# A decoder trunk on one core: other pools for the first split weights, another order at the beginning, another PSUM bank for one head

## Chip, cores and metric

The kernel runs on one core of a Trainium2 chip. The metric is the device time of one execution in microseconds (us). PE is TensorE (matrix products), ACT is ScalarE, DVE is VectorE, POOL is GpSimd; SP issues most DMAs.

## What is computed

x is 512 x 1024 in float32; there are two layers, each of a feed-forward block, a mixer (retention beside attention with a forget gate) and another feed-forward block. The reference, cut:

```python
def swiglu(h, w_in, w_out):
    gu = h @ w_in
    a, b = gu[..., :D_FF], gu[..., D_FF:]
    return (jax.nn.silu(a) * b) @ w_out
...
def reference(x, ...):
    for l in range(DEPTH):                       # DEPTH = 2, D_FF = 2816
        x = x + 0.5 * swiglu(rmsnorm(x, norm_ffn1[l]), w_ffn1_in[l], w_ffn1_out[l])
        h = rmsnorm(x, norm_mix[l])
        x = x + mixing_sublayer(h, ...)          # 4 retention heads, 8 attention heads, two gates
        x = x + 0.5 * swiglu(rmsnorm(x, norm_ffn2[l]), w_ffn2_in[l], w_ffn2_out[l])
    return rmsnorm(x, norm_final)
```

## The kernel before

**Splits.** Every float32 product is done as three products of rounded parts: an operand is split into a high part (`split`, ACT cast, L154) and the rest (DVE subtraction, L155), and PE multiplies high by high, high by low and low by high. Weights come by DMA into staging tiles (`wst_A12`, `w0`, ...), and their two parts are `wH_i`, `wL_i`. For x scaled by a norm's gain the two parts are made by `scaled` (ACT L251, DVE L252).

**A feed-forward block's first product** goes in groups of columns (`ffn_group`), each by seven block products in place of eight. x^T lies as eight tiles x0 to x7 (feature blocks), and the forms are made from the pairs (x_k, x_k+4), k = 0 to 3, by `prep_forms`: `b2_k`, `n1_k` (each a scaled tile) and the last combinations `mh_k`, `ml_k` (high and low parts of four sums `mt`, DVE L273 to L281). The steps in order are A12 times b2 into the bank Y, A11 times n1 into X, S1A11 times a sum into X, S1 into W, S3 into X, S1A11A12 times b2 into W, A22 into X; for a group of four column blocks a step is 24 matmuls at L424. A step's weight has two halves with numbers of their own: wH_0 and wH_1 are A12's, wH_2 and wH_3 A11's, wH_4 and wH_5 S1A11's, wH_6 and wH_7 S1's.

**Buffers and order.** Tiles come from pools with a fixed number of buffers for each tag; within a tag the buffers go to the tiles in program order, and a tile waits until the reader of an older one is done. `wtile` takes every fourth split weight (wH_0, wL_0, wH_4, ...) from the tag `y` with four buffers, the others from `wH` and `wL`. The list FORM_TAGS (L246) gives the tags of the 14 form tiles in the order in which `prep_forms` makes them: the last two, mh3 and ml3, are in `y`. At the very beginning FIRST_TAGS (L247) holds instead; there mh1 and one b2 tile are in `y`. The program is written in order, and a scheduler then sets each engine's instruction queue, by priorities in program order and its own estimate of times; each engine runs its queue strictly in that order.

**The beginning.** `inputs` (from L1143) transposes x on PE and copies the result from PSUM with DVE (L1156). `ffn_plain` (L521 on) does the first two column blocks without the seven-product scheme: pa and pb on PE with the weights `wH_first`, each result multiplied by R, the 1/rms of every token laid out over 128 partitions (DVE L531, L540). R goes rT (PE, L302), rowsT (DVE, L304), a write to DRAM (r_d) and a read back (R), both issued by SP. `first_forms` after it makes the forms of the first block.

**The mixer's end.** `soft` and `weigh` do the attention heads: for head h the transposed probabilities ptr, then the values po (L193 to L195), whose bank `pos[h]` has one buffer (tag `po`); ACT and DVE split the result into o, after which the next head can use the bank. Gate products pg take a bank of the tag `acc` (three buffers), as many other products do, and `pyr`, `pyf` are the outputs of both branches. pw (L1107 adds it to x) ends the mixer; as each x_k is finished, `prep_forms` runs for the next block. There are three such passages into a feed-forward block with forms: mixer to second block in layer 0, second block of layer 0 to first block of layer 1, and mixer to second block in layer 1.

Of the kernel before, what the change touches and what calls it, by code (L numbers as in the profile page):

```python
# [14 lines left out]
P = 128  # L15
T = 512
# [4 lines left out]
DFF = 2816  # L21
# [5 lines left out]
FH = 8  # L27
# [15 lines left out]
def trunk(  # L43
# [25 lines left out]
    V, S, G, PE = nc.vector, nc.scalar, nc.gpsimd, nc.tensor  # L69
# [8 lines left out]
    def st(tag, name, dt=F32):  # L78
        return sp.tile([P, T], dt, tag=tag, bufs=SLOTS[tag], name=name)

    def st2(tag, name, dt=FR):

        return sp.tile([P, 2 * T], dt, tag=tag, bufs=PAIRS[tag], name=name)
# [5 lines left out]
    def wide(name, dt=F32):  # L89
        return sp.tile([P, 10 * P], dt, tag="wide", bufs=3, name=name)  # L90
# [4 lines left out]
    def pst(tag, bufs, name):  # L95
        return ps.tile([P, T], F32, tag=tag, bufs=bufs, name=name)

    def acc(name, other=False):
        return pst("lg", 2, name) if other else pst("acc", 3, name)
# [17 lines left out]
    def gain(n, l, m):  # L117
        c = (n * DEPTH + l) * KD + m
        return gcol[:, c:c + 1]

    def ngain(n, l, m):
        c = (n * DEPTH + l) * KD + m
        return ncol[:, c:c + 1]
# [24 lines left out]
    xs = [st("x", f"x{m}") for m in range(KD)]  # L148
# [4 lines left out]
    def split(src, hi, lo, lo_eng=None):  # L153
        S.copy(hi, src)  # L154
        (lo_eng or V).tensor_tensor(out=lo, in0=src, in1=hi.bitcast(F32), op=ALU.subtract)  # L155
# [63 lines left out]
    def square(src, i):  # L219

        sq = st("r" if i < 2 else "t", "sq")
        S.activation(sq, src, AF.Square)
        if i < 2:
            sqa[i] = sq
        else:
            G.dma_start(sqa[i % 2], sq, accum_op=ALU.add)
        if i == KD - 1:
            V.tensor_tensor(out=sqa[0], in0=sqa[0], in1=sqa[1], op=ALU.add)
# [14 lines left out]

    forms = {}

    FORM_TAGS = ("xh",) * 8 + ("o",) * 4 + ("y",) * 2  # L246
    FIRST_TAGS = ("o",) * 4 + ("y",) * 2 + ("v",) * 4 + ("qk",) * 4  # L247
    tags = [None]

    def scaled(h, lo, src, g):  # L250
        S.activation(h, src, AF.Copy, scale=g)  # L251
        V.scalar_tensor_tensor(  # L252
            out=lo, in0=src, scalar=g, in1=h.bitcast(F32), op0=ALU.mult, op1=ALU.subtract
        )

    def prep_forms(n, l, k, first=False):

        if k == 0:
            tags[0] = iter(FIRST_TAGS if first else FORM_TAGS)
            forms.clear()  # L260
        x1, x2 = xs[k], xs[k + 4]
        H2 = T // 2
        b2 = st2(next(tags[0]), f"b2_{k}")
        scaled(b2[:, 0:T], b2[:, T:2 * T], x2, gain(n, l, k + 4))
        if k % 2 == 0:
            forms["n1", k // 2] = st2(next(tags[0]), f"n1_{k}")
        n1 = forms["n1", k // 2][:, (k % 2) * T:(k % 2 + 1) * T]
        scaled(n1[:, 0:H2], n1[:, H2:T], x1[:, 0:H2], ngain(n, l, k))
        b1 = st("t", "b1")
        S.activation(b1, x1, AF.Copy, scale=gain(n, l, k))  # L270
        mt = wide("mt")[:, 0:2 * T]
        m1, m2, m3, m4 = (mt[:, i * H2:(i + 1) * H2] for i in range(4))
        V.tensor_tensor(out=m1, in0=b1[:, 0:H2], in1=b1[:, H2:T], op=ALU.subtract)  # L273
        V.scalar_tensor_tensor(
            out=m2, in0=x2[:, H2:T], scalar=gain(n, l, k + 4), in1=m1, op0=ALU.mult, op1=ALU.add
        )
        V.scalar_tensor_tensor(
            out=m3, in0=x2[:, H2:T], scalar=ngain(n, l, k + 4), in1=b1[:, H2:T],
            op0=ALU.mult, op1=ALU.add,
        )  # L280
        V.scalar_tensor_tensor(  # L281
            out=m4, in0=x2[:, 0:H2], scalar=gain(n, l, k + 4), in1=m2,
            op0=ALU.mult, op1=ALU.subtract,
        )
        mh, ml = st2(next(tags[0]), f"mh{k}"), st2(next(tags[0]), f"ml{k}")
        split(mt, mh, ml)
        for q in range(2):
            def at(t, c):
                return t[:, c + q * P:c + (q + 1) * P]
            forms["b21", k, q] = at(b2, 0), at(b2, T)  # L290
            forms["b22", k, q] = at(b2, H2), at(b2, T + H2)
            forms["n11", k, q] = at(n1, 0), at(n1, H2)
            for i in range(4):
                forms[f"m{i + 1}", k, q] = at(mh, i * H2), at(ml, i * H2)
        if not first:
            square(x1, 2 * k)
            square(x2, 2 * k + 1)

    def to_dram(cols, n, nm):

# [24 lines left out]
    def rpow(sums, count, nm):  # L325
        n = sums.shape[1]
        ms, r = small([P, n], f"ms{nm}"), small([P, n], f"rs{nm}")
        V.tensor_scalar(
            out=ms, in0=sums, scalar1=1.0 / count, scalar2=EPS, op0=ALU.mult, op1=ALU.add
        )  # L330
        G.tensor_tensor(out=r, in0=ms, in1=mhalf[:, 0:n], op=ALU.pow)
        return r
# [188 lines left out]
    def ffn_plain(w, mk):  # L521

        u, sil = [], []
        cha = mk(w, 0)
        rtok = rpow(sums(), D, "x")
        R = bcast(flat(to_dram(rtok, TB, "r")), "r", "R")
        for jj in range(2):
            o = acc("pa")
            proj(o, cha[jj], xH, xL)
            t = st("t", "t1")  # L530
            V.tensor_tensor(out=t, in0=o, in1=R, op=ALU.mult)  # L531
            s = st("p", "sil")
            S.activation(s, t, AF.Silu)
            sil.append(s)
        chb = mk(w, DFF, True)
        for jj in range(2):
            o = acc("pb", True)
            proj(o, chb[jj], xH, xL)
            t = st("t", "t2")
            V.tensor_tensor(out=t, in0=o, in1=R, op=ALU.mult)  # L540
            V.tensor_tensor(out=t, in0=t, in1=sil[jj], op=ALU.mult)
            h, lo = st(U_TAGS[jj], "uH", FR), st(U_TAGS[jj], "uL", FR)
            split(t, h, lo)
            u.append((h, lo))
        first_forms()
        return u, rtok

    def lazy(make):
# [189 lines left out]
    def mix(l):  # L738
        w = w_in[l]
# [110 lines left out]
        soft, pos = {}, {}  # L850
# [38 lines left out]
        def weigh(h, j):  # L889

            p, hh = h // 2, h % 2
            pr = soft[h][0]
            n = T - j * P
            pt = pst("pt", 2, "ptr")
            for i in range(j, TB):
                o0 = (i * (i + 1) // 2 + j) * P
                PE.transpose(pt[:, (i - j) * P:(i - j + 1) * P], pr[:, o0:o0 + P], ident)
            pH, pL = st("a", "pH", FR), st("a", "pL", FR)
            split(pt[:, :n], pH[:, :n], pL[:, :n])
            if j == 0:  # L900
                pos[h] = pst("po", 1, "po")
            po = pos[h]
            vs = slice(p * P, (p + 1) * P)
            mm3(
                po[:, j * P:], fvH[j][:, vs], fvL[j][:, vs], pH[:, :n], pL[:, :n],
                j == 0, j == TB - 1,
            )
            if j == TB - 1:
                if hh == 0:
                    oH[p], oL[p] = hl("o", "o")  # L910
                r = slice(hh * 64, hh * 64 + 64)
                split(po[r], oH[p][r], oL[p][r])
# [184 lines left out]
        for k in range(KD // 2):  # L1097
# [5 lines left out]
            for jj in range(2):  # L1103
                m = k + 4 * jj
                o = acc("pw", k % 2 == 1)
# [7 lines left out]
    def sums():  # L1113
        o = small([P, TB], "sumx")
        V.tensor_tensor(out=o, in0=ssx[:, 0:TB], in1=ssx[:, TB:2 * TB], op=ALU.add)
        return o
# [26 lines left out]
    def inputs():  # L1143
        for hf in range(2):
            xi = []
            for b in range(TB):
                t = st("g", "xi")
                load(t, x[0, b * P:(b + 1) * P, hf * T:(hf + 1) * T])
                xi.append(t)
            if hf == 0:  # L1150
                gains(0, DEPTH * KD, ((0, norm_ffn1),))
            for m in range(hf * 4, hf * 4 + 4):
                o = pst("pt", 2, "xT") if m % 2 else pst("lg", 2, "xT")
                for b in range(TB):
                    PE.transpose(o[:, b * P:(b + 1) * P], xi[b][:, (m % 4) * P:(m % 4 + 1) * P], ident)
                V.tensor_copy(xs[m], o)  # L1156
                xH[m], xL[m] = hl("xh", f"xh{m}")
                scaled(xH[m], xL[m], xs[m], gain(0, 0, m))
            for b in range(TB):
                sq = st("r", "sq")  # L1160
                c = hf * TB + b
                S.activation(sq, xi[b], AF.Square, accum_out=ssx[:, c:c + 1])

    def first_forms():
        for k in range(4):
            prep_forms(0, 0, k, True)

    inputs()
    for l in range(DEPTH):
# [61 lines left out]
```

## Time and profile before

| what | value |
|---|---|
| median of 3 runs (lowest to highest) | 2232.05 us (2231.32 to 2232.57) |
| the profiled execution | 2233.17 us, of it 2231.4 us from the first to the last instruction |
| PE busy | 2169.5 us (97%), mean granted clock 0.988 |
| DVE, ACT, POOL busy | 62%, 45%, 18% |
| idle PE before a step's first Y matmul | 39.5 us in 4 places |

The sum of a change is made against 2233.17 us, the time of the execution that the trace shows; it stands 1.1 us above the median. In a row of the timeline the time behind the start is the duration, and the bracket at the end is the engine's idle time before the row and what ended it. Rows of one engine overlap by some hundredths of a us, since an instruction's start is counted while the one before it drains. PEclk in a row of windows is the granted clock: 1.00 is 2.4 GHz and 0.50 is 1.2 GHz.

### The profile page before, as it was taken

The numbers are of one execution on the slowest core, as the hardware profiler recorded it, in microseconds if no ns is written. First come the engines' busy times: TensorE is split into PE (matmuls) and PEld (weight loads), VectorE is DVE, ScalarE is ACT, GpSimd is POOL, SyncE is SP. The second block draws the span as 40 slices with busy tenths as digits, with TensorE's granted clock in tenths as the row PEclk, the third lists the DMA queues.
The fourth block names the chain that finished last, engine by engine and source line by source line (L and its number), as shares of the span: only waits on it lengthen the run. The fifth ranks groups of instructions, "written<-read, shape, count | busy, mean of one in ns | idle before, by whom it ended". The sixth has DMA issues, their size and how long they took to land.

```text
span 2231.4 us, 26468 instructions
## 1 busy us (share of the span) xinstructions
PE 2169.5 (97%) x10199; PEld 1807.5 (81%) x10199; DVE 1378.7 (62%) x1928; ACT 998.0 (45%) x1439; POOL 395.8 (18%) x330
## 2 busy tenths in 40 slices
PE   5999999999999999999989999999999999999998
PEld 4888888888878788888868888888888787888887
DVE  6666574557854765757666574656577547747564
ACT  5444353345543453525544352543454435535343
POOL 1010001454231100001010000015532321000001
PEclk8999999999999999999999999999999999999999
DMA  9366335324253645747655564353332527536441
GB/s 272 95 176 183 106 84 146 100 76 114 95 130 102 161 128 137 193 118 188 163 138 154 139 162 117 85 152 90 95 91 95 151 77 202 164 105 170 132 114 67
DMA packets 232806, 293.77 MB, mean 132 GB/s; under 512 B 11252, under 2 KB 140120, under 8 KB 232680
## 3 DMA queue, kind: packets, MB, share of 16 engines
q1 hardware_dynamic: 203240, 239.12, 34.2%
q0 software_dynamic: 29440, 52.96, 14.0%
q8 instruction: 80, 1.31, 0.2%
q14 instruction: 46, 0.38, 0.1%
HBM read 282.03 MB, written 2.15 MB: 127 GB/s over the span
## 4 chain that ended last, share of the span: by engine, by line
PE 95%; DVE 2%; ACT 1%; DMA 1%; issue 1%; SPq 0%; POOLq 0%; ACTq 0%
PE X L424 21%; PE W L424 10%; PE po L194 6%; PE po L195 6%; PE po L193 6%; PE Y L424 5%; PE pg L195 3%; PE pg L193 3%; PE pg L194 3%; PE uT L503 2%; PE po L700 1%; PE po L702 1%; PE po L701 1%; PE prq L193 1%; PE pv L212 1%; PE pv L213 1%
## 5 line engine op out<-in xcount | busy, mean ns | idle before, releaser
L154 ACT CAST wH<-A 128x1024 fp32r<-128x1024 f32 x138 | 145.3, 1053 | 179.7 <-PE po L194 51.5
L155 DVE TENSOR_TENSOR wL<-A,wH 128x1024 fp32r<-128x1024 f32 x138 | 168.5, 1222 | 81.5 <-ACT wH L154 79.1
L424 PE MATMUL X<-wL,mh 128*128 128x512 f32 (+1 forms) x552 | 206.9, 375 | 0.0
L424 PE MATMUL X<-wH,ml 128*128 128x512 f32 (+1 forms) x552 | 206.9, 375 | 0.0
L194 PE MATMUL po<-uL,wH_o 128*128 128x512 f32 x528 | 206.8, 392 | 0.0
L195 PE MATMUL po<-uH,wL_o 128*128 128x512 f32 x528 | 203.7, 390 | 0.3 <-DVE wL_o L155 0.3
L424 PE MATMUL X<-wH,mh 128*128 128x512 f32 (+1 forms) x552 | 201.0, 376 | 0.0
L193 PE MATMUL po<-uH,wH_o 128*128 128x512 f32 x528 | 199.3, 392 | 0.0
L398 POOL DMA_DIRECT2D S<-in_w_ffn_in x71 | 80.4, 1198 | 607.7 <-DMA S<-in_w_ffn_in 362.8
L424 PE MATMUL Y<-wH,b 128*128 128x512 f32 (+1 forms) x368 | 114.3, 383 | 39.5 <-ACT wH L154 39.5
L154 ACT CAST wH_o<-wst_o 128x1024 fp32r<-128x1024 f32 (+1 forms) x72 | 70.5, 981 | 135.7 <-PE po L194 107.3
L155 DVE TENSOR_TENSOR wL_o<-wst_o,wH_o 128x1024 fp32r<-128x1024 f32 (+1 forms) x72 | 81.5, 1132 | 75.5 <-ACT wH_o L154 74.2
L155 DVE TENSOR_TENSOR wL<-wst_A,wH 128x1024 fp32r<-128x1024 f32 x77 | 93.8, 1222 | 46.9 <-ACT wH L154 46.3
L154 ACT CAST wH<-wst_A 128x1024 fp32r<-128x1024 f32 x77 | 80.6, 1051 | 86.8 <-PE Y L424 17.5
L424 PE MATMUL X<-wH,n 128*128 128x512 f32 (+1 forms) x368 | 119.4, 395 | 0.0
L424 PEld LDWEIGHTS X<-wH,mh 128*128 128x128 f32 x552 | 103.9, 188 | 19.1 <-ACT e L480 0.2
L424 PEld LDWEIGHTS X<-wL,mh 128*128 128x128 f32 x552 | 103.9, 188 | 18.9
L424 PEld LDWEIGHTS X<-wH,ml 128*128 128x128 f32 x552 | 103.9, 188 | 18.9
L195 PEld LDWEIGHTS po<-uH,wL_o 128*128 128x128 f32 x528 | 99.2, 188 | 20.9 <-DVE wL_o L155 0.7
L193 PEld LDWEIGHTS po<-uH,wH_o 128*128 128x128 f32 x528 | 99.1, 188 | 21.0 <-ACT uH L154 0.4
L194 PEld LDWEIGHTS po<-uL,wH_o 128*128 128x128 f32 x528 | 99.2, 188 | 19.8
L424 PE MATMUL W<-wH,b 128*128 128x512 f32 (+1 forms) x368 | 114.5, 375 | 0.0
(314 smaller groups left out, 5545.1 us busy)
## 6 DMA issues: line engine op xcount, KB each, us to landing
A<-in_w_ffn_in SPq DMA_DIRECT2D x84, 512.0 KB, 8.1
S<-in_w_ffn_in SPq DMA_DIRECT2D x47, 512.0 KB, 4.1
S<-in_w_ffn_in POOLq DMA_DIRECT2D x47, 512.0 KB, 7.7
wst_A<-in_w_ffn_in SPq DMA_DIRECT2D x45, 512.0 KB, 5.1
wst_o<-in_w_ffn_out SPq DMA_DIRECT2D x20, 1024.0 KB, 5.4
wst_g<-in_w_in SPq DMA_DIRECT2D x16, 1024.0 KB, 5.7
wst_S<-in_w_ffn_in SPq DMA_DIRECT2D x27, 512.0 KB, 5.9
wst_S<-in_w_ffn_in POOLq DMA_DIRECT2D x27, 512.0 KB, 7.4
```

The source lines that it names most:

```text
L154: S.copy(hi, src)
L155: (lo_eng or V).tensor_tensor(out=lo, in0=src, in1=hi.bitcast(F32), op=ALU.subtract)
L193: PE.matmul(o, wh, mh, start=first, stop=False)
L194: PE.matmul(o, wh, ml, start=False, stop=False)
L195: PE.matmul(o, wl, mh, start=False, stop=last)
L212: PE.matmul(o, mvH[kk][:, bs], h[:, k], start=kk == 0, stop=False)
L213: PE.matmul(o, mvH[kk][:, bs], lo[:, k], start=False, stop=False)
L398: G.dma_start(*piece(ts, r1, c1, s), accum_op=ALU.add)
L424: last_mm[0] = PE.matmul(*args, skip_group_check=True, **kw).ins
L503: PE.transpose(o[:, b * P:(b + 1) * P], ub[b][:, j * P:(j + 1) * P], ident)
L700: PE.matmul(o, uh, hh, start=k + i == 0, stop=False)
L701: PE.matmul(o, uh, ll, start=False, stop=False)
```

## The change

- FORM_TAGS and FIRST_TAGS: b2_0 and n1_0, the first forms, take `y`; the last combinations take `o`, at the beginning `qk`.
- `prep_forms` is cut into `prep_blocks` (b2, n1) and `prep_sums` (the combinations). At the beginning the second weight of `ffn_plain`, all four `prep_blocks` and two `prep_sums` stand ahead of R; the other two `prep_sums` stand behind the pb products.
- In `inputs` the odd x tiles are copied by ACT, the even ones by DVE as before.
- The values of the last head (h = 7) take a bank of `acc` in place of the one of `po`.

```diff
-    FORM_TAGS = ("xh",) * 8 + ("o",) * 4 + ("y",) * 2
-    FIRST_TAGS = ("o",) * 4 + ("y",) * 2 + ("v",) * 4 + ("qk",) * 4
+    FORM_TAGS = ("y",) * 2 + ("xh",) * 8 + ("o",) * 4
+    FIRST_TAGS = ("y",) * 2 + ("o",) * 4 + ("v",) * 4 + ("qk",) * 4
...
-    def prep_forms(n, l, k, first=False):
-
+    def prep_forms(n, l, k):
+
+        prep_blocks(n, l, k)
+        prep_sums(n, l, k)
+        square(xs[k], 2 * k)
+        square(xs[k + 4], 2 * k + 1)
+
+    def prep_blocks(n, l, k, first=False):
...
+    def prep_sums(n, l, k):
+        x1, x2 = xs[k], xs[k + 4]
+        H2 = T // 2
         b1 = st("t", "b1")
...
         cha = mk(w, 0)
+        chb = mk(w, DFF, True)
+        for k in range(4):
+            prep_blocks(0, 0, k, True)
+        for k in range(2):
+            prep_sums(0, 0, k)
         rtok = rpow(sums(), D, "x")
...
-        chb = mk(w, DFF, True)
...
-        first_forms()
+        for k in range(2, 4):
+            prep_sums(0, 0, k)
...
-                pos[h] = pst("po", 1, "po")
+                pos[h] = acc("po") if h == FH - 1 else pst("po", 1, "po")
...
-                V.tensor_copy(xs[m], o)
+                if m % 2:
+                    S.copy(xs[m], o)
+                else:
+                    V.tensor_copy(xs[m], o)
```

The order in which the engines run changes at these places. A name is the tile and its number in the program; `<-` stands between what is written and what is read.

ACT at the end of the mixer of layer 0, before; wH_0_6178 is the high part of A12's first half, mh3 the last combination:

```order
L251 ACTIVATE n1_2_6036<-x3_84,ncol_75 128x256
L270 ACTIVATE b1_6124<-x3_84,gcol_74 128x512
L222 ACTIVATE sq_6135<-x3_84 128x512
L154 CAST wH_3_6216<-wst_A11_0_6145 128x1024
L251 ACTIVATE b2_3_6119<-x7_88,gcol_74 128x512
L222 ACTIVATE sq_6138<-x7_88 128x512
L154 CAST mh3_6131<-mt_6126 128x1024
L154 CAST wH_0_6178<-wst_A12_0_6142 128x1024
```

The same engine in the changed kernel, where the cast of wH_0 stands now; wH_wo are weights of the products pw, and b2_1 is made from x5:

```order
L222 ACTIVATE sq_5964<-x1_82 128x512
L154 CAST mh0_5877<-mt_5872 128x1024
L154 CAST wH_wo2030_6059<-wst_wo203_6056 128x1024
L154 CAST wH_0_6178<-wst_A12_0_6142 128x1024
L251 ACTIVATE b2_1_5948<-x5_86,gcol_74 128x512
L222 ACTIVATE sq_5967<-x5_86 128x512
L154 CAST mh1_5960<-mt_5955 128x1024
L154 CAST wH_wo2031_6063<-wst_wo203_6056 128x1024
```

The cast of wH_0 moved from behind the last combination of x7 to a place ahead of b2_1, 19 instructions earlier: they are those from b2_1 to mh3.

PE between the values of head 4 (po_4799) and head 5 (po_4957) in layer 0, before; lg are logits, pg_5254 a gate product:

```order
L869 MATMUL lg_4961<-k0_4766,q_4690 128x256
L870 MATMUL lg_4961<-k0_4766,q_4690 128x256
L193 MATMUL pg_5254<-xh0_2568,wH_g0120_5246 128x512
L194 MATMUL pg_5254<-xh0_2568,wH_g0120_5246 128x512
L193 MATMUL po_4799<-pH_4876,v_3899 128x256
L195 MATMUL pg_5254<-xh0_2568,wL_g0120_5247 128x512
L193 MATMUL pg_5254<-xh1_2574,wH_g0120_5246 128x512
L194 MATMUL pg_5254<-xh1_2574,wH_g0120_5246 128x512
L195 MATMUL pg_5254<-xh1_2574,wL_g0120_5247 128x512
```

PE at the same place in the changed kernel:

```order
L884 MATMUL lg_4961<-k0_4766,q_4690 128x256
L885 MATMUL lg_4961<-k0_4766,q_4690 128x256
L193 MATMUL po_4799<-pH_4876,v_3899 128x256
L194 MATMUL po_4799<-pL_4877,v_3899 128x256
L195 MATMUL po_4799<-pH_4876,v_3899 128x256
L193 MATMUL po_4799<-pH_4896,v_3902 128x128
L912 MATMUL ptr_4948<-ident_72,pr5_4779 128x128 x4
L194 MATMUL po_4799<-pL_4897,v_3902 128x128
L195 MATMUL po_4799<-pH_4896,v_3902 128x128
L912 MATMUL ptr_4972<-ident_72,pr5_4779 128x128 x3
L912 MATMUL ptr_4994<-ident_72,pr5_4779 128x128 x2
```

The 48 matmuls of the two gate products pg_5254 and pg_5281 moved from here, and from between the values of heads 5 and 6, to a place behind the first matmul of head 7's values; the `acc` buffer of those values comes ahead of theirs in the program. pyr_5178, pyf_5192 and pyr_5212 moved up relative to them.

DVE at the beginning, before, around the copy rowsT and the first use of R (t1):

```order
L252 SCALAR_TENSOR_TENSOR xh7_190<-x7_88,gcol_74,xh7_190 128x512
L304 COPY rowsT_224<-rT_222 4x128
L155 TENSOR_TENSOR wL_first_299<-w0_288,wH_first_298 128x256
L155 TENSOR_TENSOR wL_first_299<-w0_289,wH_first_298 128x256
L155 TENSOR_TENSOR wL_first_299<-w0_290,wH_first_298 128x256
L155 TENSOR_TENSOR wL_first_299<-w0_291,wH_first_298 128x256
L531 TENSOR_TENSOR t1_255<-pa_230,R_228 128x512
```

DVE there in the changed kernel:

```order
L252 SCALAR_TENSOR_TENSOR b2_2_255<-x6_87,gcol_74,b2_2_255 128x512
L252 SCALAR_TENSOR_TENSOR n1_2_258<-x2_83,ncol_75,n1_2_258 128x256
L314 COPY rowsT_296<-rT_294 4x128
L252 SCALAR_TENSOR_TENSOR b2_3_261<-x7_88,gcol_74,b2_3_261 128x512
L252 SCALAR_TENSOR_TENSOR n1_2_258<-x3_84,ncol_75,n1_2_258 128x256
L155 TENSOR_TENSOR ml0_274<-mt_268,mh0_273 128x1024
L155 TENSOR_TENSOR ml1_285<-mt_279,mh1_284 128x1024
L546 TENSOR_TENSOR t1_327<-pa_302,R_300 128x512
L155 TENSOR_TENSOR wL_first_227<-w0_216,wH_first_226 128x256
```

rowsT now has eleven operations on forms, combinations and wL_0 ahead of it that it had not, and four copies of x less; ml0 and ml1 stand ahead of the first use of R, and the low part of the second pb weight (wL_first_227) moved behind it. The buffers of the S3 loads on SP are those of `w0`, the staging tiles that wL_first reads.

## Rows read from the trace of the kernel before

**Rows 1.** waits of PE: engine, line, releaser: us in total, times, longest us

```profile
PE Y L424 <- ACT wH L154: 39.5, 4, 19.9
PE po L193 <- DVE o L155: 4.8, 2, 2.4
PE pyf L193 <- ACT o L154: 1.3, 2, 0.7
```

**Rows 2.** windows, beginning: length; PE, PEld, DVE, ACT, POOL busy; PEclk; DMA share; GB/s

```profile
36.00:56.00 20.00, 0.10 (x1) 0.00 (x0) 18.29 (x30) 8.93 (x13) 4.08 (x5) 0.58 1.00 313
56.00:60.00 4.00, 3.97 (x10) 3.16 (x11) 4.00 (x8) 2.96 (x5) 2.08 (x3) 0.55 0.65 95
```

**Rows 3.** timeline of PE, beginning: start, us, line, operation, tiles, idle before

```profile
56.03 1.22 PE L424 MATMUL Y<-wH,b 128*128 128x512 f32 x2 [19.93 <-ACT wH L154]
...
86.44 0.39 PE L424 MATMUL W<-wH,b 128*128 128x512 f32 x1
86.67 0.39 PE L424 MATMUL W<-wL,b 128*128 128x512 f32 x1
```

**Rows 4.** timeline of ACT at the beginning

```profile
53.04 1.99 ACT L154 CAST mh<-mt 128x1024 fp32r<-128x1024 f32 x2 [5.81 <-DVE mt L281]
54.94 1.04 ACT L154 CAST wH<-wst_A 128x1024 fp32r<-128x1024 f32 x1
```

**Rows 5.** timeline of DVE at the beginning

```profile
25.81 0.27 DVE L304 COPY rowsT<-rT 4x128 f32<-4x128 f32 x1
...
37.39 1.29 DVE L531 TENSOR_TENSOR t<-pa,R 128x512 f32<-128x512 f32 x2 [5.91 <-DMA R<-r_d]
...
39.20 2.35 DVE L155 TENSOR_TENSOR wL<-wst_A,wH 128x1024 fp32r<-128x1024 f32 x2
...
45.94 0.47 DVE L277 SCALAR_TENSOR_TENSOR mt<-x,ncol,b 128x256 f32<-128x256 f32 x1
```

**Rows 6.** timeline of SP: the issues of R and of the S3 loads

```profile
32.87 0.34 SPq L102 DMA_DIRECT2D R<-r_d  x1
33.30 1.81 SPq L102 DMA_DIRECT2D S<-in_w_ffn_in  x4
```

**Rows 7.** timeline of PE at the first two passages into a feed-forward block

```profile
777.21 1.22 PE L424 MATMUL Y<-wH,b 128*128 128x512 f32 x2 [5.25 <-ACT wH L154]
...
1132.08 1.22 PE L424 MATMUL Y<-wH,b 128*128 128x512 f32 x2 [9.08 <-ACT wH L154]
```

**Rows 8.** windows behind the three passages

```profile
777.21:783.00 5.79, 5.79 (x14) 4.59 (x15) 4.42 (x4) 0.00 (x0) 0.00 (x0) 0.50 1.14 286
...
1132.08:1138.00 5.92, 5.92 (x14) 4.66 (x15) 2.86 (x3) 0.00 (x0) 0.00 (x0) 0.50 0.01 3
...
1874.04:1880.00 5.96, 5.96 (x16) 4.77 (x17) 4.42 (x4) 0.21 (x1) 1.98 (x2) 0.59 1.08 336
```

**Rows 9.** timeline of ACT at the mixer's end, layer 0

```profile
751.46 0.72 ACT L251 ACTIVATE b<-x,gcol 128x512 fp32r<-128x512 f32 x1
...
772.76 0.72 ACT L251 ACTIVATE b<-x,gcol 128x512 fp32r<-128x512 f32 x1
...
776.11 1.04 ACT L154 CAST wH<-wst_A 128x1024 fp32r<-128x1024 f32 x1
```

**Rows 10.** SP there, and DMA issues: tiles, queue, times, KB, median us to landing

```profile
747.93 10.88 SPq L102 DMA_DIRECT2D wst_A<-in_w_ffn_in  x4
wst_A<-in_w_ffn_in SPq DMA_DIRECT2D x4, 512.0 KB, 3.8
```

**Rows 11.** timeline of PE, first matmul of head 6's values, both layers

```profile
630.10 0.77 PE L193 MATMUL po<-pH,v 128*128 128x512 f32 x1 [2.39 <-DVE o L155]
...
1729.53 0.47 PE L193 MATMUL po<-pH,v 128*128 128x512 f32 x1 [2.39 <-DVE o L155]
```

**Rows 12.** windows behind those waits, layer 0 and layer 1

```profile
630.00:636.50 6.50, 6.40 (x20) 5.38 (x21) 5.20 (x24) 2.60 (x9) 0.00 (x0) 0.51 0.00 0
...
1730.00:1736.00 6.00, 5.84 (x33) 5.00 (x33) 4.97 (x26) 4.18 (x11) 0.00 (x0) 1.00 0.00 0
```

More of the change, by code (lines that the diff above doesn't have):

```diff
@@ L268, in prep_forms, with at @@
         scaled(n1[:, 0:H2], n1[:, H2:T], x1[:, 0:H2], ngain(n, l, k))
+        for q in range(2):
+            def at(t, c):
+                return t[:, c + q * P:c + (q + 1) * P]
+            forms["b21", k, q] = at(b2, 0), at(b2, T)
+            forms["b22", k, q] = at(b2, H2), at(b2, T + H2)
+            forms["n11", k, q] = at(n1, 0), at(n1, H2)
+    def prep_sums(n, l, k):
+        x1, x2 = xs[k], xs[k + 4]
+        H2 = T // 2
         b1 = st("t", "b1")
@@ L289, in at @@
                 return t[:, c + q * P:c + (q + 1) * P]
-            forms["b21", k, q] = at(b2, 0), at(b2, T)
-            forms["b22", k, q] = at(b2, H2), at(b2, T + H2)
-            forms["n11", k, q] = at(n1, 0), at(n1, H2)
             for i in range(4):
                 forms[f"m{i + 1}", k, q] = at(mh, i * H2), at(ml, i * H2)
-        if not first:
-            square(x1, 2 * k)
-            square(x2, 2 * k + 1)
     def to_dram(cols, n, nm):
@@ L1162, in inputs @@
                 S.activation(sq, xi[b], AF.Square, accum_out=ssx[:, c:c + 1])
-    def first_forms():
-        for k in range(4):
-            prep_forms(0, 0, k, True)
     inputs()
```

## The prediction

> **What bounds the kernel now.** PE is busy nearly all the time, so I read first where it waits. Of the table of its waits one line counts: Y at L424, the first matmul of a feed-forward block with forms, stood idle for 39.5 us in four places behind an ACT cast [rows 1]. The timeline gives the places: 19.93 us at the beginning [rows 3], 5.25 and 9.08 us at the first two passages [rows 7], and so 39.5 - 19.93 - 5.25 - 9.08 = 5.24 us at the third. Next come the values of the attention heads, 4.8 us in two places [rows 1, 11].
>
> Each wait on Y has a second price. In the stretch behind it the granted clock is 1.2 GHz: 0.50 over 5.79 us, 0.50 over 5.92 us and 0.59 over 5.96 us behind the three passages [rows 8], 0.55 in the 4 us behind the first wait [rows 2]. Work done there at half speed would have taken half of it: 2.9 + 3.0 + 2.4 = 8.3 us lost behind the passages.
>
> What ends the wait is wH_0, the cast of the first half of A12. ACT is not busy with other things: the cast stands behind mh3 in its queue, at 776.11 [rows 9], though its load was issued at 747.93 and took 3.8 us [rows 10]. It is the buffer that holds it back: wH_0 and wL_0 need two of the four `y` buffers, and mh3 and ml3 come first in the program. At the beginning the same holds with mh1: its sums were waited for 5.81 us on DVE, and wH_0 follows at 54.94 [rows 4]; DVE is 18.29 us busy in those 20 us [rows 2].
>
> **The passages.** In the new order wH_0 stands on ACT ahead of x5's b2, which began at 751.46 [rows 9]: 25 us earlier. What is late next? The last product pw ends PE's work at 777.21 - 5.25 = 771.96. Then 18 Y matmuls (k = 0 to 2) and 8 of X need nothing of x7, which is 26 matmuls of some 0.227 us (starts at 86.44 and 86.67 [rows 3]) = 5.9 us, to 777.9. x7's b2_3 began on ACT at 772.76 [rows 9] and needs the low part on DVE, some 3 us of DVE work (its sums, wL_3, its own), so about 776. The 48 matmuls of A12 and A11 last 10.9 us, to 782.8; S1A11's wH_4 needs the buffer of wH_0, free after the 15th matmul (775.4), a cast of 1.04 and a subtraction of 1.2 us, so 778 to 779, and mh3 and ml3 follow by 780. Nothing is late by this, at the first two passages within 0.3 us by the same reading. The load of A12 was the last thing that could hold the cast: 747.93 + 3.8 = 751.7 [rows 10], about when the cast's turn comes. ACT's queue behind it (b2_1, mh1, one pw weight) moves by the cast's 1.04 us, and ACT is idle for more than that before 772. The gain: 19.57 us idle and 8.3 us of clock, 27.9 us; with up to 1 us left at each passage, 24.5 to 28. I take **27.5 us**, since the cover (10.9 us) is twice what is late.
>
> **The beginning.** Here the bound changes hands. In the new order 12 Y matmuls stand among those of pa and pb, and x1 and x3 are copied by ACT ahead of the first weights, so PE starts pa some 1 us later (two copies of 0.6). PE was done with pb at 56.03 - 19.93 = 36.1 [rows 3], with the first pb 24 matmuls earlier, at 30.6; plus 1 and 12 x 0.227 us that is 34.4. rowsT stood at 25.81 [rows 5]; with eleven operations more (some 5.4 us by the starts of rows 5) and four copies of 0.6 fewer, and waits for ACT, it slips to 29 or 30. The second pb's low weight now stands on DVE behind t1, which waits for R. R's read was issued at 32.87 [rows 6], 7 us after rowsT, and had landed by 37.39 [rows 5]. If that time was the backlog of the DMA queues, R comes at about the same time; if it was the chain's own, 11.6 us from rowsT, it comes some 3.9 us later, at 41.3. I take the first: the small write stands behind weight loads, and these are issued as before. So PE is idle from 34.4 to about 38.4 (R, t1 and one quarter of wL_first).
>
> From R on DVE is the bound. Up to the low part of S1's first weight it has 16 operations of 512 columns (37.39: two in 1.29, some 0.6 each), 7 of 1024 (39.20: two in 2.35, some 1.13 each) and 12 of 256 (0.47, some 0.38 each) [rows 5]. By the spacing of starts that is 9.6 + 7.9 + 4.6 = 22.1 us, by durations 24.2: to 59.5 or 61.6. PE has 72 matmuls for that time (the second pb, the rest of A12, A11, half of S1A11), to 38.4 + 16.3 = 54.7, and waits again. From there 58 matmuls of S1A11, W and S3 follow, 13.2 us, to 72.7 or 74.8, with mh2, ml3 and the S3 weights ready in time: the S3 loads, issued at 33.30 [rows 6], now wait for wL_first, so some 6 us, and are first used at 67. Before, the same point is W's first matmul on b2 at 86.44 [rows 3]: 11.6 to 13.7 us gained. The second wait (5 us) will cost some clock, 0 to 3 us as behind the passages [rows 8]; the first one lies before a stretch that DVE bounds anyway. ACT's four copies and DVE's four fewer are in these starts. Ends: 6 (R late, clock lost) to 14. I take **12 us**.
>
> **The heads.** The change frees the bank between heads 6 and 7, where the trace shows no wait: 2.39 us stand before head 6's values, in both layers [rows 11]. It also takes 48 gate matmuls (10.9 us) from between heads 4 and 6 and puts them behind head 7's first one. A hand-over of the bank then costs PE 2.4 us twice (heads 4 to 5 and 5 to 6) in place of once, +2.4 us. Some comes back: the gates now stand where pyf waits, 0.65 us in each layer [rows 1], and where other small waits of some 0.6 us stand. Net +1.1 us a layer. The clock decides the rest: behind the same 2.39 us it was 0.51 over 6.50 us in layer 0 and 1.00 in layer 1 [rows 12], so one layer has lost 3.2 us already. Neither: 2.2 - 3.2 = -1 us; one of two: +2.2; both: +5.4. I take one of two, **+2 us**.
>
> **The sum.** 2233.2 - 27.5 - 12 + 2 = 2195.7 by the profiled execution; less 1.1 us to the median, 2194.6, rounded to 2194.5 us.
>
> **Rivals.**
> (a) The heads' clock falls in both layers, with two sparse hand-overs 5 us apart in place of one. Then +5.4 in place of +2: 2198. For it: layer 0 fell behind a single gap [rows 12]. Against: layer 1 did not.
> The Trainium skill, page "TensorE: Matmul & The Clock Gate", section "A second HAM failure mode: psum-queue depth-cycling", says that short idle times between groups of matmuls, when banks are cycled, are enough to make the clock go back and forth. That speaks for (a) and so against this part of the change; the trace agrees in layer 0 and not in layer 1.
> (b) R is the bound of the beginning: its chain takes its own 11.6 us from rowsT and ends at 41.3, and the clock is lost too. 6 us gained in place of 12: 2200.5. For it: DVE's rowsT is late for certain, being in a strict queue. Against: the backlog.
> (c) All is hidden better: 14 us at the beginning, no fall of the clock at the heads (-1), 28 at the passages: 2233.2 - 28 - 14 - 1 - 1.1 = 2189.
> (d) Slower. ACT's cast of wH_0 now stands ahead of b2_1, mh1 and the last pw weight, and waits for A12's load. That weight is needed 24 matmuls before 771.96, at 766.5, and its cast has some 9 us of room if the load lands at 751.7. A load that lands later than that holds PE back us for us, the last pw products and the forms with it; to eat up the 37.5 us at three passages it would have to land 9 + 13 us later than now. The median landing takes 3.8 us [rows 10], so this is unlikely; from that point the time would be above 2232, say 2240.
> (e) The change doesn't do what it says: another tile of `y` holds wH_0 as long. The order of ACT speaks against it, since the cast stands ahead; then 2232.
>
> **How the numbers follow.** Forecast 0.46 (2190 to 2199 on its own), (a) 0.17, (b) 0.16, (c) 0.15, (d) 0.03, (e) 0.03. A difference of 0.2% (4.5 us) is about what a measurement can tell from none. (a) to (c) and the forecast are all faster by over 1%: 0.94; same 0.03 from (e); slower 0.03 from (d). The range goes from a little beyond (c) to beyond (b) with a us or two lost at the passages and the heads: 2186 to 2207.
>
> **What would show each step.** Right: no wait over 0.5 us before Y at the three passages and PEclk 1.00 there; at the beginning two waits, of 3 to 5 us each, the first ended by a low part of wL_first behind R, the second by wL on DVE, and W's b2 matmul near 73; waits of about 2.4 us before the values of heads 5 and 6 and none before pyf. Wrong: a wait on Y of several us again, R after 40, or the two stretches of the heads together longer than before by over 6 us.

## Result and the profile after

The changed kernel takes 2210.57 us (median of 4 runs, 2206.28 to 2210.84) beside 2232.31 us for the kernel before: a ratio of 0.9898, 95% interval 0.9881 to 0.9915. It is 22 us faster, not 38, and lies above the top of the range, 2207.

I cut both traces at the same matmuls: the last change from a po to a Y product in the first feed-forward block of the mixer's layer, the first matmul of head 4's values, the last pw product, and the next change from po to Y behind it. Ends of stretches in us:

| stretch | before | after | gained |
|---|---|---|---|
| beginning, to head 4's first value, layer 0 | 608.30 | 596.25 | 12.05 |
| from there to the last pw, layer 0 | 771.95 | 768.70 | -8.80 |
| first passage | 854.25 | 842.38 | 8.62 |
| second passage (1122.99 to 1216.99 before, 1111.13 to 1192.88 after) | | | 12.25 |
| mixer of layer 1 (1383.99 to 1868.79, 1359.88 to 1853.72) | | | -9.04 |
| third passage, to 2005.55 and 1983.14 | | | 7.34 |

Passages 28.2 us (27.5 forecast), beginning 12.05 (12 forecast), heads -17.84 (-2 forecast). One term failed. These are single traces: in the eight runs below that keep the new beginning as it is, head 4's first value comes between 594.6 and 597.4 us, so the 12.05 us may be 11 to 14.

Waits of PE in the changed kernel (releaser: us in total, times, longest us):

```profile
PE pg L193 <- ACT wH_g L154: 7.5, 4, 4.5
...
PE ptr L912 <- DVE pr L902: 3.9, 2, 2.0
```

Y, first with 39.5 us in [rows 1], is no longer in the list, and the wait of po on o is gone too. New are pg, the gate product, behind the cast of its weight, and ptr, the transposing of probabilities, behind DVE. Windows behind the passages, as in [rows 8] (length; PE, PEld, DVE, ACT, POOL busy; PEclk; DMA share; GB/s):

```profile
769.00:775.00 6.00, 6.00 (x28) 4.99 (x27) 5.96 (x10) 3.76 (x5) 2.25 (x2) 1.00 0.98 305
1111.00:1117.00 6.00, 6.00 (x28) 4.99 (x27) 6.00 (x10) 4.65 (x7) 1.71 (x2) 1.00 0.28 46
1854.00:1860.00 6.00, 6.00 (x28) 4.97 (x27) 5.96 (x10) 3.78 (x5) 1.41 (x2) 1.00 1.00 309
```

PE is busy throughout at a granted clock of 1.00 (2.4 GHz), with 28 matmuls in 6 us where [rows 8] have 14 or 16.

The beginning, PE, DVE and SP, as in [rows 3, 5, 6] (start, us, engine, line, operation, idle before and releaser):

```profile
36.68 0.50 PE L195 MATMUL pb<-xh,wL_first 128*128 128x512 f32 x1 [0.85 <-DVE wL_first L155]
...
57.09 0.79 PE L434 MATMUL W<-wL,mh 128*128 128x512 f32 x1 [3.80 <-DVE wL L155]
...
73.03 0.39 PE L434 MATMUL W<-wH,b 128*128 128x512 f32 x1
```

```profile
30.20 0.27 DVE L314 COPY rowsT<-rT 4x128 f32<-4x128 f32 x1
...
35.60 0.69 DVE L546 TENSOR_TENSOR t<-pa,R 128x512 f32<-128x512 f32 x1 [1.80 <-DMA R<-r_d]
```

```profile
32.41 0.34 SPq L102 DMA_DIRECT2D R<-r_d  x1
```

The mixers in one row each, before and then after (windows view, columns as above), from the last change of po to Y in the block ahead to the last pw. The two kernels stand 12.05 us apart at 254.40 as they do at head 4's first value, so all that the mixer loses in layer 0 it loses behind that:

```profile
254.40:771.95 517.55, 513.86 (x2397) 427.66 (x2396) 315.99 (x522) 229.54 (x362) 142.67 (x113) 0.99 0.40 111
1383.99:1868.79 484.80, 480.94 (x2335) 403.19 (x2333) 300.04 (x511) 218.12 (x353) 142.71 (x113) 1.00 0.41 112
```

```profile
242.35:768.70 526.35, 516.68 (x2398) 428.50 (x2398) 318.24 (x524) 230.37 (x363) 143.69 (x113) 0.99 0.39 109
1359.88:1853.72 493.84, 486.00 (x2335) 405.71 (x2335) 300.57 (x513) 217.75 (x354) 143.38 (x113) 0.99 0.40 110
```

The second number is PE's busy time. With as many matmuls, layer 0 has 9.67 us idle (526.35 - 516.68) where it had 3.69, and 2.82 us more busy; layer 1 has 7.84 idle where it had 3.86, and 5.06 more busy. More busy time for the same matmuls means that more of them ran at the lower clock, as the windows below show. The large waits, PE's timeline of the changed kernel in both layers:

```profile
608.73 0.69 PE L912 MATMUL ptr<-ident,pr 128*128 128x128 f32 x2 [2.02 <-DVE pr L902]
...
652.12 0.50 PE L193 MATMUL pg<-xh,wH_g 128*128 128x512 f32 x1 [4.48 <-ACT wH_g L154]
...
1696.22 0.44 PE L912 MATMUL ptr<-ident,pr 128*128 128x128 f32 x2 [1.86 <-DVE pr L902]
...
1736.81 0.50 PE L193 MATMUL pg<-xh,wH_g 128*128 128x512 f32 x1 [2.47 <-ACT wH_g L154]
```

Behind all four the clock fell (windows; PEclk is the third number from the end):

```profile
609.00:616.00 7.00, 7.00 (x23) 5.49 (x23) 5.35 (x25) 4.12 (x13) 0.00 (x0) 0.57 0.01 2
652.00:655.00 3.00, 2.43 (x6) 1.62 (x7) 2.89 (x4) 2.68 (x6) 2.33 (x2) 0.60 0.31 101
1696.00:1700.00 4.00, 3.67 (x11) 2.64 (x12) 3.63 (x19) 1.84 (x6) 0.00 (x0) 0.64 0.00 0
1736.00:1741.00 5.00, 3.67 (x9) 2.65 (x10) 3.77 (x5) 3.90 (x6) 3.64 (x3) 0.71 0.67 202
```

### The profile page after: what moved, and what is told of

It reads as the page before. It is cut to its first block, busy times and chain, and to the rows that moved or that the text cites. A ratio compares the mean times of both kernels' runs of the same rounds, so it can differ in the third digit from the quotient of the medians.

```text
span 2209.1 us, 26483 instructions
## 1 busy us (share of the span) xinstructions
PE 2170.7 (98%) x10199; PEld 1805.7 (82%) x10199; DVE 1372.6 (62%) x1924; ACT 996.0 (45%) x1443; POOL 397.6 (18%) x330
## 4 chain that ended last, share of the span: by engine, by line
PE 93%; DVE 3%; DMA 2%; ACT 1%; issue 0%; SPq 0%; POOLq 0%; ACTq 0%; DVEq 0%
PE X L434 21%; PE W L434 11%; PE po L193 6%; PE po L194 6%; PE po L195 6%; PE Y L434 5%; PE pg L195 3%; PE pg L193 2%; PE pg L194 2%; PE uT L513 2%; PE po L715 1%; PE po L717 1%; PE po L716 1%; DMA wst_g<-in_w_in 1%; PE prq L193 1%; PE pv L212 1%
## 5 line engine op out<-in xcount | busy, mean ns | idle before, releaser
L434 PE MATMUL X<-wH,n 128*128 128x512 f32 (+1 forms) x368 | 113.7, 379 | 0.0
## 6 DMA issues: line engine op xcount, KB each, us to landing
wst_g<-in_w_in SPq DMA_DIRECT2D x16, 1024.0 KB, 10.8
```

Source lines behind the costliest of these rows:

```text
L434: last_mm[0] = PE.matmul(*args, skip_group_check=True, **kw).ins
```

## Experiments

### The three parts apart

**x6_forms_only**: the kernel before with only `FORM_TAGS` in the new order.

```diff
-    FORM_TAGS = ("xh",) * 8 + ("o",) * 4 + ("y",) * 2
+    FORM_TAGS = ("y",) * 2 + ("xh",) * 8 + ("o",) * 4
```

> The kernel before with one part of the change: in the order of the forms' pools the two y pairs come first. Theory A (the three parts add up, and the passages' part is worth what the landmarks of the changed kernel say, 8.6 + 12.3 + 7.3 = 28.2 us): 2231.4 - 28.2 = 2203 us, with no wait before Y at the three passages, and the beginning (first wait on Y 19.9 us) and the heads (2.39 us before the values of head 6) as before. Rival B (part of what the passages gain in the changed kernel belongs to the shifted beginning or to the emptied bank): 2207 to 2215.

Measured: 2205.57 us, ratio 0.9888 [0.9874, 0.9903], 26.5 us less than before's 2232.02. By the landmarks the three passages gained 9.2, 12.3 and 7.0 us, 28.5 us together, which is Theory A's 28.2, though the median stands 2.6 us above its 2203.

**x7_begin_only**: the changed kernel with `FORM_TAGS` and head 7's bank as before.

> The changed kernel with the forms' order and the bank of head 7 as before, so that the new beginning alone is left. Theory A (it is worth the 12.05 us by which head 4's first value came earlier, and all of it reaches the end): 2231.4 - 12.05 = 2219.4 us, with the three waits on Y at the passages (5.2, 9.1, 5.2 us) back. Rival B (an earlier beginning is given back at the first passage, where loads and casts then come no earlier): 2222 to 2231.

Measured: 2220.09 us, ratio 0.9950 [0.9933, 0.9966], 11.9 us less, as Theory A has it. Its waits on Y at the passages are 5.25, 9.09 and 5.26 us.

**x2_po_only**: the kernel before with only head 7's values in an acc bank.

```diff
-                pos[h] = pst("po", 1, "po")
+                pos[h] = acc("po") if h == FH - 1 else pst("po", 1, "po")
```

> The kernel before with one part of the change alone: head 7's values take a bank of acc. Theory A: 2232 + 17.8 = 2250 us (2245 to 2254), with a wait of 2 to 5 us before a gate product behind head 7 in each layer. Theory B: 2232 us, within 3.

Measured: 2249.34 us, ratio 1.0076 [1.0059, 1.0093], 17.9 us more than before's 2231.42, as Theory A has it.

**x1_po_back**: the changed kernel without that one line.

> The changed kernel with one part undone: head 7's values take the single bank of po again, as before. By position the trace of the changed kernel puts a loss of 8.8 us on the heads of layer 0 and 9.0 us on those of layer 1 (first matmul of head 4's values to the last pw product). Theory A, the loss comes from the bank of head 7, whose place in the acc order pushes the gate products back: both stretches return to 163.65 and 161.0 us or so, time 2210.6 - 17.8 = 2193 us (2190 to 2196). Theory B, the loss comes from the rest of the change (weights and forms arriving at other times, other DMA traffic under the heads): it stays near 2210, at most 3 us less.

Measured: 2193.65 us, ratio 0.9829 [0.9814, 0.9843], as Theory A has it. So the parts add up: -26.5 - 11.9 + 17.9 = -20.5, beside -21.7 for all three. The one line on the bank takes back nearly half of what the other two give.

### Why the gate weight is late

In the changed kernel, gate(1,2) comes to stand behind head 7's values in the rotation of acc banks. SP and ACT in layer 0, timelines of the changed kernel:

```profile
626.82 8.02 SPq L102 DMA_DIRECT2D S<-in_w_ffn_in  x8
634.93 9.38 SPq L102 DMA_DIRECT2D wst_g<-in_w_in  x2
```

```profile
632.44 1.05 ACT L154 CAST wH_g<-wst_g 128x1024 fp32r<-128x1024 f32 x1 [4.15 <-PE pg L194]
...
651.03 1.04 ACT L154 CAST wH_g<-wst_g 128x1024 fp32r<-128x1024 f32 x1 [9.13 <-DMA wst_g<-in_w_in]
```

and in the kernel before, SP and ACT:

```profile
620.03 0.37 SPq L102 DMA_DIRECT2D wst_g<-in_w_in  x1
...
645.29 5.83 SPq L102 DMA_DIRECT2D S<-in_w_ffn_in  x8
```

```profile
617.23 1.05 ACT L154 CAST wH_g<-wst_g 128x1024 fp32r<-128x1024 f32 x1
```

Before, gate(1,2)'s second cast at 617.23 emptied a staging tile, and the next gate weight, gate(0,4), was issued at 620.03, 25 us ahead of the eight loads of the next feed-forward block's sums (S1, S3). Now that cast comes at 632.44, which is 27 us later counted from head 4's first value, and the issue at 634.93, behind the eight. Its 1 MB lands beside the last of them and beside the eight that POOL accumulates on top (DMA issues of the changed kernel there: tile, queue, times, KB, median us to landing; then the window, whose last two numbers are DMA share and GB/s):

```profile
S<-in_w_ffn_in POOLq DMA_DIRECT2D x8, 256.0 KB, 7.5
wst_g<-in_w_in SPq DMA_DIRECT2D x2, 1024.0 KB, 16.0
```

```profile
635.00:651.00 16.00, 12.06 (x50) 8.88 (x49) 4.73 (x6) 2.00 (x2) 6.02 (x6) 1.00 1.06 260
```

16.0 us from 634.93 is 650.9, and the cast begins at 651.03; the mean DMA share over that time is 1.06. Two causes are possible: the tile that comes free late, and the sixteen loads. The next two runs separate them without touching PE's order in the mixer.

**x10_no_aside**: S1 and S3 of layer 0's second block go to their usual places, so the sixteen loads come later.

```diff
-                rtok, w_i[l], groups, "a" if pi == 0 and (first or which == 2) else None, u
+                rtok, w_i[l], groups, "a" if pi == 0 and first else None, u
```

> The changed kernel, but the sums S1 and S3 of the second feed-forward block of each layer are loaded into their usual places and not into four a tiles ahead of time. So the eight loads that stand before the gate weights in SP's queue in the heads come behind them, with their eight accumulating loads; TensorE's order from head 4 to the last pw product is that of the changed kernel, matmul for matmul. Theory A (the gate weight comes late because its load is issued behind and lands beside those sixteen loads): the waits of 4.48 and 2.47 us before pg are gone or under 1 us, and the way from head 4's first value to the last pw product is 5 to 8 us shorter in layer 0 than in the changed kernel (172.45 us) and 3 to 5 in layer 1. Rival B (it comes late because its staging tile is freed late, whatever else is in the queue): the waits stay, 3.5 to 4.5 and 2 to 2.5 us. At the passages behind, S1 and S3 now come late by either theory; what that costs is not forecast, so the total is 2200 to 2215 by A, 2209 to 2225 by B.

Layer 1's second block has a call of its own, which this edit doesn't reach, so the expectation for layer 1 was wrong and layer 1 serves as the control. ACT, SP and windows of x10_no_aside (the gate weight's landing, then the two mixers):

```profile
641.76 1.05 ACT L154 CAST wH_g<-wst_g 128x1024 fp32r<-128x1024 f32 x1
...
1740.58 1.04 ACT L154 CAST wH_g<-wst_g 128x1024 fp32r<-128x1024 f32 x1 [7.99 <-DMA wst_g<-in_w_in]
```

```profile
634.74 11.36 SPq L102 DMA_DIRECT2D wst_g<-in_w_in  x2
```

```profile
634.74:642.00 7.26, 7.06 (x31) 5.40 (x30) 2.39 (x4) 2.14 (x3) 0.92 (x1) 1.00 0.46 144
...
242.69:762.58 519.89, 514.65 (x2398) 427.68 (x2398) 319.42 (x521) 230.33 (x363) 137.59 (x106) 0.99 0.36 102
1364.55:1859.47 494.92, 486.97 (x2336) 406.45 (x2335) 300.48 (x513) 217.85 (x354) 143.65 (x113) 0.99 0.40 110
```

The load is issued at the same time, 634.74, so its place behind the eight in SP's queue cost it nothing; it meets a DMA share of 0.46 where the changed kernel has 1.06, and is cast 7.0 us later with no wait on a DMA. So the wait before pg is gone, and layer 0 is 6.46 us shorter (526.35 to 519.89). In layer 1 the loads stand where they stood, pg waits 3.33 us, and the mixer is 1.08 us longer than in the changed kernel (494.92 beside 493.84): so far apart are two traces of the same order. The whole is slower, 2214.91 us (0.9928 [0.9913, 0.9942]): the first passage now waits for S1's and S3's parts and costs 10.8 us more (762.58 to 847.06 beside 768.70 to 842.38).

**x12_no_aside_last**: the mirror, layer 1 alone.

```diff
-            todo = ffn_in(rtok, w_i[l], groups, None if pi else "a", u)
+            todo = ffn_in(rtok, w_i[l], groups, None, u)
```

> The mirror of x10_no_aside, whose edit reached layer 0's second feed-forward block alone (there the wait before pg went and 6.46 us with it; in layer 1, whose loads it left as they were, a wait of 3.33 us stayed). Here layer 1's S1 and S3 go to their usual places and layer 0's loads stay as in the changed kernel. TensorE's order up to layer 1's last pw product is that of the changed kernel. Theory A (the gate weight's load is late because of the sixteen loads around it): in layer 0 the wait before pg is 4 to 5 us as in the changed kernel, in layer 1 (2.47 us there) it is gone or under 1 us, and the way to the last pw product is 2.5 to 5 us shorter than its 493.84 us. Rival B (x10's layer 0 differed by chance or by something else): layer 1's wait stays at 2 us or more. The passage behind then pays for late S1 and S3, as in x10 some 8 to 13 us: total 2214 to 2220.

PE and the window of layer 1 in x12_no_aside_last:

```profile
649.11 0.80 PE L193 MATMUL pg<-xh,wH_g 128*128 128x512 f32 x1 [4.59 <-ACT wH_g L154]
```

```profile
1357.37:1846.34 488.97, 483.72 (x2336) 404.71 (x2335) 301.52 (x510) 217.98 (x354) 137.54 (x106) 1.00 0.37 102
```

Layer 0's wait is 4.59 us, layer 1's is gone, and layer 1 is 4.87 us shorter (493.84 to 488.97); its passage pays 8.6 us for that, and the whole takes 2212.17 us (0.9918 [0.9901, 0.9934]). The sixteen loads are what makes the gate weight late, in both layers, and with the clock behind the wait that is 6.46 + 4.87 = 11.3 of the 17.84 us, to within a us or so for each layer. The tile that comes free late causes no wait before pg by itself; it is what moves the load in among them. Whether SP's eight or POOL's eight weigh more was not tried.

### Another bank does not give what it frees

**x3_lg7**: head 7's values in one of the two lg banks instead, so that the gates keep their place.

```diff
-                pos[h] = acc("po") if h == FH - 1 else pst("po", 1, "po")
+                pos[h] = acc("po", True) if h == FH - 1 else pst("po", 1, "po")
```

> The changed kernel with head 7's values in a bank of the logits (lg, two buffers) in place of acc: the values still have a bank of their own, but take no place in the acc order, and the gate products stand between heads 4 and 6 as before the change. Theory A (the acc order is what costs): 2193 us, within 3 of the kernel with the single bank. If a bank of its own costs by itself, for example because head 7's products now run into other work: near 2210.

Measured: 2209.63 us (0.9899 [0.9885, 0.9914]), 16 us slower than with one bank. The late gate weight isn't there, and the miss has a cause of its own. PE and ACT in x3_lg7:

```profile
623.71 0.44 PE L912 MATMUL ptr<-ident,pr 128*128 128x128 f32 x2 [0.99 <-DVE pr L902]
627.99 0.79 PE L193 MATMUL po<-pH,v 128*128 128x512 f32 x1 [3.85 <-ACT pH L154]
628.58 0.63 PE L193 MATMUL pyr<-y,wH_wo 128*128 128x512 f32 x1
```

```profile
622.95 1.28 ACT L1099 ACT_TABLE_LOAD   x1
...
627.37 0.94 ACT L154 CAST pH<-ptr 128x512 fp32r<-128x512 f32 x2
```

With its bank free from the start, head 7's first product stands on PE ahead of the pyr and pyf products that are its cover in x1_po_back, where twelve pyr stand right before it. It needs the cast pH, and that stands on ACT behind a table load and, from 624.24 on, the sigmoids of the gates: ptr ended at 624.15, pH began at 627.37. The Trainium skill, page "Perfetto Trace Analysis", section "Tensor Engine Instruction (MATMUL, LD_WEIGHTS)", says that ACT takes its instructions strictly in order; these rows agree, with 3.2 us. From head 4's first value to the last pw the two layers take 170.46 and 170.80 us, beside 162.23 and 162.54 in x1_po_back; 5.3 us of the difference in each are idle and 3.0 more busy, which is the clock.

**x5_lg6**: the bank for head 6, where the 2.39 us are, head 7 as before.

```diff
-                pos[h] = acc("po") if h == FH - 1 else pst("po", 1, "po")
+                pos[h] = acc("po", True) if h == FH - 2 else pst("po", 1, "po")
```

> The changed kernel with head 7's values in the one po bank as before, and head 6's, before which the 2.39 us stand, in one of the two lg banks. The gate products keep the place that they had before. Theory A (the 2.39 us are the hand-over of the one bank from head 5 to head 6; another bank removes them and nothing else changes): 2 x 2.4 us less than x1_po_back's 2193.7, so 2187 to 2189. Rival B (with a bank of its own the first product of head 6 waits for its own probabilities at the same place, or an lg bank taken so long holds up the logits or pyr): the gap stays or moves, 2193 to 2210.

Measured: 2195.83 us (0.9846 [0.9829, 0.9862]), beside 2193.65 of x1_po_back: nothing gained, as Rival B has it. PE and ACT in x5_lg6, then ACT and DVE in the kernel before:

```profile
616.32 0.50 PE L193 MATMUL po<-pH,v 128*128 128x512 f32 x1 [1.52 <-ACT pH L154]
617.81 0.79 PE L194 MATMUL po<-pL,v 128*128 128x512 f32 x1 [0.99 <-DVE pL L155]
```

```profile
614.00 1.05 ACT L154 CAST wH_wo<-wst_wo 128x1024 fp32r<-128x1024 f32 x1 [0.69 <-PE pg L194]
...
615.68 0.97 ACT L154 CAST pH<-ptr 128x512 fp32r<-128x512 f32 x2
```

```profile
626.92 1.05 ACT L154 CAST wH_wo<-wst_wo 128x1024 fp32r<-128x1024 f32 x1 [0.93 <-PE pg L194]
627.99 0.58 ACT L154 CAST o<-po 64x512 fp32r<-64x512 f32 x1
628.59 0.97 ACT L154 CAST pH<-ptr 128x512 fp32r<-128x512 f32 x2
```

```profile
628.00 1.23 DVE L155 TENSOR_TENSOR wL_wo<-wst_wo,wH_wo 128x1024 fp32r<-128x1024 f32 x1 [1.69 <-ACT wH_wo L154]
629.26 0.69 DVE L155 TENSOR_TENSOR o<-po,o 64x512 fp32r<-64x512 f32 x1
```

In both, ACT stands in a weight's cast, which waits for the last gate product to free its buffer; behind it come the cast that empties the bank and, 0.6 us later, head 6's own pH. DVE makes the low parts in the same order, head 6's pL last (629.98; 617.07 in x5_lg6). With the bank out of the way PE waits for pH and pL, 1.52 + 0.99 = 2.51 us in place of 2.39. So [rows 11] show the bank, but it is the middle one of three splits in a row on ACT and DVE (the weight's, o's, head 6's own): freeing it brings the third no sooner. In x9_fill_po (below) ACT is done with that weight at 612.36, ahead of head 5's last product, and po waits 0.29 us for o.

### The place of the gate products

**x4_fill**: the changed kernel with gate(1,2) written out between heads 6 and 7, ahead of head 7's values in the rotation.

```diff
-        interleave(step(6) + step(7) + step(8), [])
+        interleave(step(6) + step(7), gate(1, 2))
+        interleave(step(8), [])
```

> The changed kernel with head 7's values in acc, but the two gate products of that stretch are written among heads 6 and 7 in the program, ahead of head 7's values, so that they come first in the acc order; all 48 matmuls stand between heads 4 and 5 on PE. Theory A: most of the 17.8 us comes back, 2193 to 2199 us, since only the hand-over from head 5 to 6 is left without filling, as it was before, 2.4 us a layer; no wait of over 1 us before the next gate weight. Theory B: 2210.

Measured: 2188.55 us (0.9807 [0.9792, 0.9822]), 22.0 us less than the changed kernel and 4 below Theory A's range: the 2.4 us that it left to the hand-over are 0.29 us in the trace.

**x9_fill_po**: the same with all heads in the one po bank.

> The changed kernel with all heads' values in the one po bank as before, and the products gate(1,2) written between heads 6 and 7 so that they still stand between heads 4 and 5. It differs from x4_fill only in head 7's bank, and from x1_po_back only in where the 48 gate products stand. Theory A (the place of the 48 gate products is all that matters, and the freed bank gains nothing): 2188.5, the same as x4_fill within 2 us. Rival B (the freed bank by itself is worth what the change meant it to be, and the place of the gate products nothing): 2193.7, the same as x1_po_back. Between them: both have a share.

Measured: 2187.30 us (0.9804 [0.9789, 0.9819]). Theory A holds: the freed bank is worth nothing, and the place of 48 products is worth 6.4 us against x1_po_back (22.0 by x4_fill against the changed kernel). The mixers of x9_fill_po:

```profile
242.26:755.83 513.57, 510.96 (x2399) 425.86 (x2398) 316.17 (x524) 230.47 (x363) 142.12 (x113) 1.00 0.41 112
1346.98:1830.80 483.82, 481.09 (x2336) 403.67 (x2335) 305.04 (x513) 217.96 (x354) 143.85 (x113) 1.00 0.41 112
```

2.61 and 2.73 us are idle, less than before, and the clock is 1.00 in both.

### The copies of x

**x8_copy_dve** and **x11_best_dve**: x1_po_back and x9_fill_po with all eight copies on DVE.

```diff
-                if m % 2:
-                    S.copy(xs[m], o)
-                else:
-                    V.tensor_copy(xs[m], o)
+                V.tensor_copy(xs[m], o)
```

> x1_po_back with all eight copies of x out of PSUM on DVE again, so that of the new beginning only the new order of the forms' steps is left. Theory A (DVE is the bound of the beginning, four copies of some 0.6 us taken from it are gained): up to 2.4 us slower than x1_po_back, 2194 to 2196, W's wait for its low weight from DVE (3.28 us there) 1 to 2.4 us later. Rival B (the copies on ACT hold the first products back by 1 us and more, and DVE has room for them ahead of R): 1 to 2 us faster, 2192 to 2193.

> x9_fill_po with all eight copies of x on DVE. Theory A of x8_copy_dve: up to 2.4 us slower than x9_fill_po (2187.3), 2188 to 2190. Rival B: 2185.5 to 2186.5.

Measured: 2193.55 us (x1_po_back 2193.65) and 2187.03 us (x9_fill_po 2187.30). The copies' engine makes no difference, so neither theory holds: what counts in the beginning is the new order with its pools. x11_best_dve is the fastest kernel of all, 0.9803 [0.9789, 0.9818], not to be told from x9_fill_po.

## The prediction, point by point

**Passages: right.** 27.5 us forecast, 28.2 by the landmarks and 26.5 for this part alone. No wait on Y and a clock of 1.00, as said. The late load of A12, rival (d), was a wait of 0.46 us on ACT.

**Beginning: right in the sum, with other parts.** W's b2 matmul starts at 73.03, forecast 72.7 to 74.8; 12.05 us gained, 11.9 alone. But rowsT was later by 4.4 us (30.20) and R was multiplied earlier, at 35.60 instead of 37.39: the write and read of R took 5.4 us from rowsT, not 11.6. So the 11.6 us were not the chain's own, and rival (b) falls; that a backlog held them up before fits the DMA share from rowsT to R's read, 0.89 then and 0.62 now. The first wait was 0.85 us and not 4, the second 3.80 and not 5 to 7; PE came to the second one at 53.29. The second wait ended at 57.09, 2.4 to 4.5 us ahead of the forecast, and the way from there to W took 15.9 us and not 13.2, with the clock at 0.50 from 57.09 to 62.00. The two errors nearly cancel, so that 73.03 lies in the range is partly luck.

**Heads: wrong, and this is the whole miss.** +2 us forecast (-1 to +5.4), +17.84 measured, far beyond rival (a) as well. The step that failed is "the gates now stand where pyf waits ... Net +1.1 us a layer". It moved 48 products on PE's queue alone, as filler that could stand anywhere. But these products also empty a weight's buffer: later products, a later cast (27 us, counted from head 4), a staging tile freed later, and the next gate weight's load amid sixteen others. x10_no_aside and x12_no_aside_last put 11.3 us on that. At the beginning the prediction followed R through SP's queue and the transfers around it; for the moved gates it did not.

The other 17.84 - 11.3 = 6.5 us are what the forecast meant to price. The rows of layer 0 in x10_no_aside and of layer 1 in x12_no_aside_last divide them, beside the kernel before: 2.9 us more idle and 3.6 us more busy, which is the clock. That is nearest to rival (a), +5.4, whose sum was 2.2 us of waits and 3.2 of clock; in the changed kernel the clock fell in both layers, to 0.57 over 7 us and 0.64 over 4. The waits are not where (a) put them. None of 2.4 us stands before the values of heads 5 and 6; PE waits for probabilities that DVE scales, 2.02 and 1.86 us, and for smaller things. Without gate products between heads 4 and 6 the softmax has no cover, and one of its steps is slower. DVE and POOL of the changed kernel:

```profile
607.16 1.52 DVE L902 TENSOR_SCALAR pr<-pr,rl 128x512 f32<-128x512 f32 x1
```

```profile
607.13 1.26 POOL L873 TENSOR_TENSOR diag<-neg,mask 128x512 f32<-128x512 f32 x1 [5.48 <-DVE rl L901]
```

The same scaling takes 0.49 us in x9_fill_po (at 611.04), where POOL does nothing beside it. So 1.0 of the 2.02 us is this meeting of DVE and POOL; in layer 1 the scaling takes 1.35 us. In x9_fill_po, with the products back between heads 4 and 5, neither the meeting nor the wait is there.

**"A hand-over of the bank costs 2.4 us": not a price of the bank.** x5_lg6 shows that the same time is lost with the bank free, and x9_fill_po that the hand-over costs 0.29 us where the weight's split is over by then. So 2.4 us couldn't be carried to heads 4 to 5.

**The clock behind such a wait: left open.** The prediction read the fall in layer 0 and none in layer 1 as evidence for and against rival (a). The same wait of about 2.39 us stands in both layers of six traces here, and the clock fell behind eight of the twelve: in layer 0 alone in the kernel before, x6_forms_only and x7_begin_only, in layer 1 alone in x8_copy_dve, in both in x1_po_back and x3_lg7. So it isn't a matter of the layer, and what decides it these runs don't show. The rule cited with rival (a), of the Trainium skill's page "TensorE: Matmul & The Clock Gate", section "A second HAM failure mode: psum-queue depth-cycling", is borne out only in part: the clock fell in both layers of the changed kernel, but behind waits for probabilities and for a weight, not for a bank. In x9_fill_po three short waits (0.40, 0.93 and 0.29 us within 612 to 618) left it at 1.00, so short waits between groups were not enough there.

Without the heads the sum would have been 2192.6 (2233.2 - 27.5 - 12 - 1.1), and x1_po_back takes 2193.65.

## What to carry to other kernels

Where tiles rotate through a pool, giving one more tile to it moves every later user back, and with a moved product go its weight's cast, the staging tile that the cast frees, and the moment at which the next load meets the other transfers; follow it through all four before calling it filler. A wait that the profile puts on a buffer may be the queue of the engines that empty it: read what they did just before, and whether the next input would be ready if the buffer were free. Before buying a bank, try to move the work that could cover the wait: here 48 products in another place were worth 6.4 us, and the bank nothing.

## What was not expected of the hardware

The same 1 MB weight load, issued at 634.9 and 634.7 us, took 16.0 us to land beside sixteen loads of 256 KB and was cast within 7.0 us without them. DVE's scaling of a 128x512 tile takes 0.5 us alone; in all 35 places of these traces where it began with or during POOL's `diag`, it took 0.9 to 1.6 us and ended 0.3 us after POOL. Where DVE began 0.1 us first (x12_no_aside_last, 606.35), it took 0.49 us and `diag` 1.50 in place of 1.26. And a wait of the same 2.39 us was followed by a lower clock eight times out of twelve, 0.50 over 3 us in layer 0 of x1_po_back and 1.00 in the same place of x8_copy_dve, so a single trace tells little of what a wait costs by the clock.
